# Product tiles of a pair in PE's column halves, with 16 KB stores held back behind loads

## The chip, the cores and the metric

The kernel runs on one core of one Trainium2 chip. Times are device microseconds (us) of that core. "Before" and "after" have four runs each; the experiments ran in three batches, each with its own runs of the kernel before on the same chip. A ratio is the mean time of one kernel's fast runs over the mean of the other's fast runs of the same rounds, so it is not quite the ratio of the medians quoted beside it.

## The reference

Sixteen batches of a product with the second factor transposed, in 32-bit floats:

```python
def setup_inputs():
    batch, m, k, n = 16, 512, 512, 512
    return {"a": randn(batch, m, k), "b": randn(batch, n, k)}   # float32

def reference(a, b):
    return np.matmul(a, b.transpose(0, 2, 1)).astype(np.float32)
```

Each batch reads 2 x 1 MB and writes 1 MB: 33.55 MB in, 16.78 MB out.

## The kernel before

Engines go by the names of the profile: PE is TensorE, which multiplies matrices, ACT is ScalarE, DVE is VectorE, SP is SyncE. SBUF and PSUM are the core's memories; what PE makes goes to PSUM. Batches go in eight pairs, 0 to 7. A load (2 MB, 16 KB per partition) brings one factor of both batches of a pair. DVE casts it to bf16, PE transposes 128 x 128 blocks into PSUM (`tp`), ACT and DVE copy these to SBUF (`ta`, `tb`), PE makes the products in `ps`, ACT copies them to an output ring `ob`, and SP stores them. There are seven load buffers (2 MB) and seven output buffers (1 MB, called halves here: half n is half of pair n // 2). ACT also issues the loads, all but load 1; all stores are issued by SP. The parts that matter:

```python
NL = 7                              # load buffers of 2 MB
NO = 7                              # output buffers of 1 MB
ob = sbuf("ob", [P, NO, J, N], f32)

def landed(n):                      # store n has landed
    return s_st[n % NO], 16 * (n // NO + 1)

def store(n):                       # 1 MB, 8 KB per partition
    nc.sync.wait_ge(s_out, n + 1)
    nc.sync.dma_start(out[n].rearrange("(p j) n -> p j n", j=J), ob[:, n % NO]
                      ).then_inc(landed(n)[0], 16)
...
nc.sync.wait_ge(s_ld[0], 32)        # no store before load 7 has landed
for n in range(batch - 1):
    store(n)
...
for u in range(pairs):              # ACT, in this order
    for ko in range(KO):            # transposes of pair u to ta
        nc.scalar.wait_ge(s_ta, KO * u + ko + 1)
        ...                         # two copies of 512 columns
    for n in (2 * u + NL, 2 * u + NL + 1):
        if n < 2 * pairs:
            load(n, nc.scalar)
    for e in range(2):
        n = 2 * u + e
        if n >= NO:
            nc.scalar.wait_ge(*landed(n - NO))      # output buffer free
        for j in range(J):
            ...                     # ob <- ps, one copy of 512 columns
...
for e in range(2):                  # PE, products of pair u
    for jj in range(0, J, 2):
        ...
        nc.tensor.matmul(ps[:, j, :],                        # 128 rows of batch e
                         ta[:, ko, (e * J + j) * P:(e * J + j + 1) * P],
                         tb[...][:, :, e * HP:(e + 1) * HP], ...)
```

The order on ACT matters below: the copies of pair u+1's transposes stand behind the output copies of pair u, and so behind the wait for an output buffer.

Of the kernel before, what the change touches and what calls it, by code (L numbers as in the profile page):

```python
# [10 lines left out]
def kernel(  # L11
# [6 lines left out]
    nc = tc.nc  # L18
    P = 128
    batch, M, K = a.shape  # L20
    _, N, _ = b.shape
    J = M // P
    KO = K // P
    HP = P // 2
    HK = K // 2
    pairs = batch // 2
    f32 = mybir.dt.float32
    bf16 = mybir.dt.bfloat16
    NL = 7
    NO = 7  # L30



    def sbuf(name, shape, dtype):
        return ctx.enter_context(nc.sbuf_tensor(name, shape, dtype))

    def sem(name):
        return tc.alloc_semaphore(name)

    with tc.tile_critical(no_gpsimd_drain=True):  # L40
        ident = sbuf("ident", [P, P], bf16)
        one = sbuf("one", [P, 1], f32)
        ld = sbuf("ld", [P, NL, 2 * J, K], f32)
        ha, wa, hb, wb = (
            sbuf(name, [P, 2 * J, HK], bf16) for name in ("ha", "wa", "hb", "wb")
        )
        ta = sbuf("ta", [P, KO, 2 * J * P], bf16)
        tb = sbuf("tb", [P, KO, 2 * J * P], bf16)
        ob = sbuf("ob", [P, NO, J, N], f32)
        tp = ctx.enter_context(nc.psum_tensor("tp", [P, 4, 2 * J, P], bf16))  # L50
        ps = ctx.enter_context(nc.psum_tensor("ps", [P, 4, N], f32))

        s_set = sem("s_set")
        s_ld = [sem(f"s_ld{i}") for i in range(NL)]
        s_st = [sem(f"s_st{i}") for i in range(NO)]

        s_go = sem("s_go")
        s_wa = sem("s_wa")
# [6 lines left out]
        s_ea = sem("s_ea")  # L65
        s_eb = sem("s_eb")
        s_mm = sem("s_mm")
        s_pv = sem("s_pv")
        s_out = sem("s_out")
# [5 lines left out]
            out=ident[:], in_=ident[:], compare_op=mybir.AluOpType.not_equal, fill=1.0,  # L75
# [6 lines left out]
        def load(n, engine):  # L82
            u, slot = n // 2, n % NL
            src = (a if n % 2 == 0 else b)[2 * u:2 * u + 2].rearrange(
                "e (p j) k -> (e p) j k", j=2 * J
            )
            engine.dma_start(ld[:, slot], src).then_inc(s_ld[slot], 16)

        def landed(n):
            return s_st[n % NO], 16 * (n // NO + 1)  # L90

        def store(n):
            nc.sync.wait_ge(s_out, n + 1)
            nc.sync.dma_start(
                out[n].rearrange("(p j) n -> p j n", j=J), ob[:, n % NO]
            ).then_inc(landed(n)[0], 16)

        load(0, nc.scalar)
        load(1, nc.sync)
        for n in range(2, NL):  # L100
            load(n, nc.scalar)

        for n in range(2 * pairs):
            nc.gpsimd.wait_ge(s_ld[n % NL], 16 * (n // NL + 1)).then_inc(s_go, 1)  # L104

        nc.sync.wait_ge(s_ld[0], 32)
        for n in range(batch - 1):
            store(n)

        def taker(engine):  # L110
            return lambda s, n: engine.wait_ge(s, n).then_inc(s, -n)  # L111
# [5 lines left out]
        take = taker(nc.vector)  # L117
# [3 lines left out]
        with nc.Fori(0, pairs, engines=[dve]) as u:  # L121
            for x, (h, w, s_c, s_w) in enumerate(
                ((ha, wa, s_ca, s_wa), (hb, wb, s_cb, s_wb))
            ):
                src = ld[:, bass.ds((u * 2 + x) % NL, 1)].rearrange("p o j k -> p (o j) k")
                take(s_go, 1)
                if x == 0:
# [4 lines left out]
                    out=h[:, J:, :], in_=src[:, J:, :HK]  # L132
                ).then_inc(s_c, 1)
                nc.vector.tensor_copy(out=w[:], in_=src[:, :, HK:]).then_inc(s_w, 1)  # L134
            for ko in range(KO):
# [5 lines left out]
                if ko == 1:  # L141
# [3 lines left out]
                    out=tb[:, ko, :],  # L145
                    in_=tp[:, 2 + ko % 2].rearrange("k j p -> k (j p)"),
# [6 lines left out]
        for u in range(pairs):  # L153
            for ko in range(KO):
                nc.scalar.wait_ge(s_ta, KO * u + ko + 1)
                for e in range(2):
                    c = nc.scalar.copy(  # L157
                        out=ta[:, ko, e * J * P:(e + 1) * J * P].rearrange(
                            "k (j p h) -> k j p h", j=J, h=2
                        ),  # L160
                        in_=tp[:, ko % 2, :, e * HP:(e + 1) * HP].rearrange(
                            "k (h j) p -> k j p h", h=2
                        ),
                    )
                c.then_inc(s_ea, 1)


            for n in (2 * u + NL, 2 * u + NL + 1):
                if n < 2 * pairs:
                    load(n, nc.scalar)  # L170
            for e in range(2):
                n = 2 * u + e
                if n >= NO:
                    nc.scalar.wait_ge(*landed(n - NO))
                for j in range(J):
                    nc.scalar.wait_ge(s_mm, J * n + j + 1)
                    c = nc.scalar.copy(  # L177
                        out=ob[:, n % NO, j, :].rearrange("m (p j) -> m p j", j=2 * J),
                        in_=ps[:, j, :].rearrange("m (j p) -> m p j", j=2 * J),
                    )  # L180
                    if e == 0:
                        c.then_inc(s_pv, 1)
                    elif j in (0, J - 1):
                        c.then_inc(s_out, 1)


        pe = nc.tensor.engine
        take = taker(nc.tensor)
        with nc.Fori(0, pairs, engines=[pe]):
            with nc.Fori(0, 2, engines=[pe]):  # L190

                for x, (h, s_c, s_t, s_e) in enumerate(
                    ((ha, s_ca, s_ta, s_ea), (hb, s_cb, s_tb, s_eb))
                ):
                    take(s_c, 1)
                    for g in range(2):
                        take(s_e, 1)
                        for j in range(2 * J):
                            t = nc.tensor.transpose(  # L199
                                tp[:, 2 * x + g, j, :], h[:, j, g * P:(g + 1) * P], ident[:]  # L200
                            )
                            if x == 1 and g == 0 and j == 0:
                                t.then_inc(s_da, 1)
                        t.then_inc(s_t, 1)



            for e in range(2):
                for jj in range(0, J, 2):
                    if e == 1:  # L210
                        take(s_pv, 2)
                    for kk in range(0, KO, 2):
                        for j in (jj, jj + 1):
                            for ko in (kk, kk + 1):
                                if (e, jj, j) == (0, 0, 0) and ko >= 2:
                                    nc.tensor.wait_ge(s_ea, ko - 1)
                                    nc.tensor.wait_ge(s_eb, ko - 1)
                                t = nc.tensor.matmul(  # L218
                                    ps[:, j, :],
                                    ta[:, ko, (e * J + j) * P:(e * J + j + 1) * P],  # L220
                                    tb[:, ko, :].rearrange("k (j p) -> k j p", j=2 * J)[
                                        :, :, e * HP:(e + 1) * HP
                                    ],
                                    start=(ko == 0),
                                    stop=(ko == KO - 1),
                                )
                            if kk == KO - 2:
                                t.then_inc(s_mm, 1)



    with tc.tile_critical(sync_engine=act, no_gpsimd_drain=True):
        for n in range(batch - NO, batch - 1):
            nc.scalar.wait_ge(*landed(n))
    waits = nc.cur_bb.bb.instructions[-1]
    last = nc.sync.dma_start(
        out[batch - 1].rearrange("(p j) n -> p j n", j=J), ob[:, (batch - 1) % NO]
    )
    tc.add_manual_dep(
        last.ins,  # L240
        waits.name,
# [33 lines left out]
```

## Time and profile before

| | before |
|---|---|
| time, median of 4 runs | 124.92 us (124.88 to 124.99) |
| moved | 50.34 MB, mean 409 GB/s over the span |
| PE busy | 73% of the span |
| DMA | nine tenths or more busy in nearly every slice |

Read such a page from the bottom of the hardware up: when the DMA row is full and no engine is, bytes set the time, and an engine matters only if it comes so late that the DMA has nothing to do. These lines of the page are groups of instructions (count | busy us, mean ns of one | idle before, with its cause) and, last, DMA issues (count, KB each, median us from issue to landing):

```profile
L218 PE MATMUL ps<-tb,ta 128*128 128x512 bf16 x256 | 57.8, 379 | 0.5
...
L218 PEld LDWEIGHTS ps<-tb,ta 128*128 128x128 bf16 x256 | 24.1, 98 | 30.6 <-issue 4.0
...
out_dram<-ob SPq DMA_DIRECT2D x16, 1024.0 KB, 25.6
```

From the table of waits of the kernel before (us in total, times, longest):

```profile
ACT ob L177 <- DMA out_dram<-ob: 3.8, 2, 3.1
```

A store takes a median of 25.6 us to land, and yet ACT waits only 3.8 us for one: stores queue deeply, and the ring of seven halves covers it.

### The profile page before, as it was taken

The page shows a single profiled execution, that of the slowest core. Times are in us where ns is not written, and L with a number is a line of the kernel's source. Part 1 is how long each engine was busy: PE and PEld are TensorE (multiplying, and loading weights), DVE is VectorE, ACT ScalarE, POOL GpSimd, SP SyncE. Part 2 cuts the span into 40 slices and gives each one's busy share as a digit, 9 for nine tenths or more (in the row PEclk, how much of TensorE's full clock was granted, in tenths as well). Part 3 has the DMA queues.
Part 4 walks back from the last instruction along what each step waited for, and adds up shares of the span by engine and source line. Part 5 has one row for each costly group of instructions (what it writes and reads, how often), then busy time and mean ns, then how long its engine had stood idle before and what let it go on. Part 6 is the DMA issues. An engine that isn't in the chain of part 4 may idle for free. (4 is left out here: it accounts for less than half of the span.)

```text
span 123.1 us, 2235 instructions
## 1 busy us (share of the span) xinstructions
PE 90.1 (73%) x768; PEld 54.7 (44%) x768; DVE 67.9 (55%) x96; ACT 67.9 (55%) x130; POOL 0.7 (1%) x6
## 2 busy tenths in 40 slices
PE   0000089999999899989998999999699936997000
PEld 0000078447734764575477447644564425542000
DVE  0000598992896589388918983871987039600000
ACT  0400064567945966696589468855865184666000
POOL 2000000000000000000000000000000000000000
PEclk9999999999999999999999999999999999999965
DMA  4999999999999998999999999999999999999991
GB/s 144 394 426 431 447 437 431 426 431 426 426 431 426 426 405 373 453 399 437 407 429 426 463 405 442 437 415 434 423 418 458 399 426 423 431 429 423 426 431 45
DMA packets 4610, 50.34 MB, mean 409 GB/s; under 512 B 513, under 2 KB 513, under 8 KB 513
## 3 DMA queue, kind: packets, MB, share of 16 engines
q10 hardware_dynamic: 2160, 31.46, 60.6%
q1 hardware_dynamic: 2448, 18.88, 36.4%
q14 instruction: 2, 0.01, 0.0%
HBM read 33.55 MB, written 16.78 MB: 409 GB/s over the span
## 5 line engine op out<-in xcount | busy, mean ns | idle before, releaser
L218 PE MATMUL ps<-tb,ta 128*128 128x512 bf16 x256 | 57.8, 379 | 0.5
L177 ACT COPY ob<-ps 128x512 f32<-128x512 f32 x64 | 34.3, 590 | 26.3 <-PE ps L218 22.5
L157 ACT COPY ta<-tp 128x512 bf16<-128x512 bf16 x64 | 33.0, 613 | 15.5 <-PE tp L199 15.0
L218 PEld LDWEIGHTS ps<-tb,ta 128*128 128x128 bf16 x256 | 24.1, 98 | 30.6 <-issue 4.0
L199 PE MATMUL tp<-ident,ha 128*128 128x128 bf16 x256 | 18.5, 224 | 18.8 <-PEq L111 18.3
L199 PEld LDWEIGHTS tp<-ident,ha 128*128 128x128 bf16 x256 | 15.8, 100 | 22.3 <-issue 20.6
L144 DVE COPY tb<-tp 128x1024 bf16<-128x1024 bf16 x32 | 21.2, 685 | 3.6 <-DVEq L111 3.6
L199 PE MATMUL tp<-ident,hb 128*128 128x128 bf16 x256 | 17.5, 223 | 3.8 <-PEq L111 3.5
L199 PEld LDWEIGHTS tp<-ident,hb 128*128 128x128 bf16 x256 | 15.3, 100 | 5.0 <-issue 4.8
L130 DVE CAST ha<-ld 128x1024 bf16 x8 | 5.5, 690 | 14.6 <-POOLq L104 13.8
L139 DVE COPY ha<-wa 128x2048 bf16<-128x2048 bf16 x8 | 5.5, 691 | 12.4 <-DVEq L111 12.4
L130 DVE CAST hb<-ld 128x1024 bf16 x8 | 5.5, 689 | 8.4 <-DVEq L111 8.4
L134 DVE CAST wa<-ld 128x2048 bf16 x8 | 9.8, 1220 | 0.0
L134 DVE CAST wb<-ld 128x2048 bf16 x8 | 9.8, 1220 | 0.0
L131 DVE CAST hb<-ld 128x1024 bf16 x8 | 5.5, 687 | 0.0
L131 DVE CAST ha<-ld 128x1024 bf16 x8 | 5.5, 687 | 0.0
L143 DVE COPY hb<-wb 128x2048 bf16<-128x2048 bf16 x8 | 5.5, 684 | 0.0
L152 ACT ACT_TABLE_LOAD x1 | 1.3, 1283 | 4.1 <-issue 4.1
L74 POOL TENSOR_SCALAR_AFFINE_SELECT ident<-ident 128x128 bf16<-128x128 bf16 x1 | 0.3, 292 | 0.2 <-POOL ident L72 0.2
L72 POOL MEMSET ident<- 128x128 bf16 x1 | 0.2, 204 | 0.5 <-SPq L40 0.5
L152 ACT COPY one<-const-float32-1.0 128x1 f32<-128x1 f32 x1 | 0.2, 191 | 0.0
L259 POOL MEMSET const-bfloat16-1.0<- 128x1 bf16 x1 | 0.1, 102 | 0.0
(3 smaller groups left out, 0.3 us busy)
## 6 DMA issues: line engine op xcount, KB each, us to landing
ld<-in_a_dram ACTq DMA_DIRECT2D x8, 2048.0 KB, 29.3
out_dram<-ob SPq DMA_DIRECT2D x16, 1024.0 KB, 25.6
ld<-in_b_dram ACTq DMA_DIRECT2D x7, 2048.0 KB, 27.1
ld<-in_b_dram SPq DMA_DIRECT2D x1, 2048.0 KB, 12.6
```

What stands on the lines that cost most here:

```text
L74: nc.gpsimd.affine_select(out=ident[:], in_=ident[:], compare_op=mybir.AluOpType.not_equal, fill=1.0, base=0, pattern=[[-1, P]], channel_m ...
L130: nc.vector.tensor_copy(out=h[:, :J, :], in_=src[:, :J, :HK])
L131: nc.vector.tensor_copy(out=h[:, J:, :], in_=src[:, J:, :HK]).then_inc(s_c, 1)
L134: nc.vector.tensor_copy(out=w[:], in_=src[:, :, HK:]).then_inc(s_w, 1)
L139: nc.vector.tensor_copy(out=ha[:], in_=wa[:]).then_inc(s_ca, 1)
L143: nc.vector.tensor_copy(out=hb[:], in_=wb[:]).then_inc(s_cb, 1)
L144: nc.vector.tensor_copy(out=tb[:, ko, :], in_=tp[:, 2 + ko % 2].rearrange("k j p -> k (j p)"),).then_inc(s_eb, 1)
L152: nc.scalar.copy(out=one[:], in_=nc.const_aps.tensor(1.0, (P, 1), f32))
L157: c = nc.scalar.copy(out=ta[:, ko, e * J * P:(e + 1) * J * P].rearrange("k (j p h) -> k j p h", j=J, h=2), in_=tp[:, ko % 2, :, e * HP:(e ...
L177: c = nc.scalar.copy(out=ob[:, n % NO, j, :].rearrange("m (p j) -> m p j", j=2 * J), in_=ps[:, j, :].rearrange("m (j p) -> m p j", j=2 * J),)
L199: t = nc.tensor.transpose(tp[:, 2 * x + g, j, :], h[:, j, g * P:(g + 1) * P], ident[:])
L218: t = nc.tensor.matmul(ps[:, j, :], ta[:, ko, (e * J + j) * P:(e * J + j + 1) * P], tb[:, ko, :].rearrange("k (j p) -> k j p", j=2 * J)[:, ...
```

## The change

The intent is stores of 16 KB per partition instead of 8 KB. For that one partition of `ob` must hold eight consecutive output rows, so both batches of a pair have to be in one product tile: batch 0 in output rows 0 to 63, batch 1 in rows 64 to 127. PE computes them as two products of 64 rows in its two column halves. A pair then leaves as one store of 2 MB, except where the ring of seven halves wraps and at the end. Each of the first four pairs' stores is held until load 2u+8 has landed. Core of the diff, cut:

```diff
+    NS = 5
+    STORES = []
+    for u in range(pairs):
+        if 2 * u % NO == NO - 1 or u == pairs - 1:
+            STORES += [(2 * u,), (2 * u + 1,)]
+        else:
+            STORES += [(2 * u, 2 * u + 1)]
...
-        nc.sync.wait_ge(s_ld[0], 32)
-        for n in range(batch - 1):
-            store(n)
+        for n, halves in enumerate(STORES[:-1]):
+            late = 2 * (halves[0] // 2) + 8
+            if late < 2 * pairs:
+                nc.sync.wait_ge(s_ld[late % NL], 16 * (late // NL + 1))
+            nc.sync.wait_ge(s_out, halves[-1] + 1)
+            store(n).then_inc(landed(n)[0], 16)
...
-                for e in range(2):
-                    c = nc.scalar.copy(out=ta[:, ko, e * J * P:(e + 1) * J * P]..., in_=...)
+                c = nc.scalar.copy(out=ta[:, ko, :], in_=tp[:, ko % 2]...)
...
+                            for e in range(2):
+                                half = slice(e * HP, (e + 1) * HP)
                                 t = nc.tensor.matmul(
-                                    ps[:, j, :],
-                                    ta[:, ko, (e * J + j) * P:(e * J + j + 1) * P],
-                                    tb[:, ko, :]...[:, :, e * HP:(e + 1) * HP],
+                                    ps[half, j % 4, :],
+                                    ta[:, ko, j * P + e * HP:j * P + (e + 1) * HP],
+                                    tb[:, ko, :]...[:, :, half],
```

The resulting stores are (0,1) (2,3) (4,5) (6) (7) (8,9) (10,11) (12,13) (14) (15), by halves.

More of the change, by code (lines that the diff above doesn't have):

```diff
@@ L29 @@
     NL = 7
+    W = 2 * J
     NO = 7
+    NS = 5
[5 more added lines that the diff above has]
+            STORES += [(2 * u, 2 * u + 1)]
+    OF = {h: n for n, halves in enumerate(STORES) for h in halves}
     def sbuf(name, shape, dtype):
@@ L48 @@
         tb = sbuf("tb", [P, KO, 2 * J * P], bf16)
-        ob = sbuf("ob", [P, NO, J, N], f32)
+        ob = sbuf("ob", [P, NO * J, N], f32)
         tp = ctx.enter_context(nc.psum_tensor("tp", [P, 4, 2 * J, P], bf16))
@@ L54 @@
         s_ld = [sem(f"s_ld{i}") for i in range(NL)]
-        s_st = [sem(f"s_st{i}") for i in range(NO)]
+        s_st = [sem(f"s_st{i}") for i in range(NS)]
         s_go = sem("s_go")
@@ L89, in landed @@
         def landed(n):
-            return s_st[n % NO], 16 * (n // NO + 1)
+            return s_st[n % NS], 16 * (n // NS + 1)
         def store(n):
-            nc.sync.wait_ge(s_out, n + 1)
-            nc.sync.dma_start(
-                out[n].rearrange("(p j) n -> p j n", j=J), ob[:, n % NO]
-            ).then_inc(landed(n)[0], 16)
+            halves = STORES[n]
+            u, lo = halves[0] // 2, halves[0] % 2 * J
+            at = halves[0] % NO * J
+            return nc.sync.dma_start(
+                out[2 * u:2 * u + 2].rearrange("e (p w) n -> (e p) w n", w=W)[
+                    :, lo:lo + len(halves) * J, :
+                ],
+                ob[:, at:at + len(halves) * J],
+            )
         load(0, nc.scalar)
@@ L155 @@
                 nc.scalar.wait_ge(s_ta, KO * u + ko + 1)
-                for e in range(2):
-                    c = nc.scalar.copy(
-                        out=ta[:, ko, e * J * P:(e + 1) * J * P].rearrange(
-                            "k (j p h) -> k j p h", j=J, h=2
-                        ),
-                        in_=tp[:, ko % 2, :, e * HP:(e + 1) * HP].rearrange(
-                            "k (h j) p -> k j p h", h=2
-                        ),
-                    )
+                c = nc.scalar.copy(
+                    out=ta[:, ko, :], in_=tp[:, ko % 2].rearrange("k j p -> k (j p)")
+                )
                 c.then_inc(s_ea, 1)
@@ L170 @@
                     load(n, nc.scalar)
-            for e in range(2):
-                n = 2 * u + e
-                if n >= NO:
-                    nc.scalar.wait_ge(*landed(n - NO))
-                for j in range(J):
-                    nc.scalar.wait_ge(s_mm, J * n + j + 1)
-                    c = nc.scalar.copy(
-                        out=ob[:, n % NO, j, :].rearrange("m (p j) -> m p j", j=2 * J),
-                        in_=ps[:, j, :].rearrange("m (j p) -> m p j", j=2 * J),
-                    )
-                    if e == 0:
-                        c.then_inc(s_pv, 1)
-                    elif j in (0, J - 1):
-                        c.then_inc(s_out, 1)
+            for j in range(W):
+                h = 2 * u + j // J
+                if j % J == 0 and h >= NO:
+                    nc.scalar.wait_ge(*landed(OF[h - NO]))
+                nc.scalar.wait_ge(s_mm, W * u + j + 1)
+                c = nc.scalar.copy(
+                    out=ob[:, h % NO * J + j % J, :].rearrange("m (p j) -> m p j", j=W),
+                    in_=ps[:, j % 4, :].rearrange("m (j p) -> m p j", j=W),
+                )
+                if j < J:
+                    c.then_inc(s_pv, 1)
+                elif j in (J, W - 1):
+                    c.then_inc(s_out, 1)
         pe = nc.tensor.engine
@@ L204 @@
                         t.then_inc(s_t, 1)
-            for e in range(2):
-                for jj in range(0, J, 2):
-                    if e == 1:
-                        take(s_pv, 2)
-                    for kk in range(0, KO, 2):
-                        for j in (jj, jj + 1):
-                            for ko in (kk, kk + 1):
-                                if (e, jj, j) == (0, 0, 0) and ko >= 2:
-                                    nc.tensor.wait_ge(s_ea, ko - 1)
-                                    nc.tensor.wait_ge(s_eb, ko - 1)
-                                t = nc.tensor.matmul(
-                                    ps[:, j, :],
-                                    ta[:, ko, (e * J + j) * P:(e * J + j + 1) * P],
-                                    tb[:, ko, :].rearrange("k (j p) -> k j p", j=2 * J)[
-                                        :, :, e * HP:(e + 1) * HP
-                                    ],
+            for jj in range(0, W, 2):
+                if jj >= J:
+                    take(s_pv, 2)
+                for kk in range(0, KO, 2):
+                    for j in (jj, jj + 1):
+                        for ko in (kk, kk + 1):
+                            if j == 0 and ko >= 2:
+                                nc.tensor.wait_ge(s_ea, ko - 1)
+                                nc.tensor.wait_ge(s_eb, ko - 1)
+                            for e in range(2):
+                                half = slice(e * HP, (e + 1) * HP)
+                                t = nc.tensor.matmul(
+                                    ps[half, j % 4, :],
+                                    ta[:, ko, j * P + e * HP:j * P + (e + 1) * HP],
+                                    tb[:, ko, :].rearrange("k (j p) -> k j p", j=W)[:, :, half],
                                     start=(ko == 0),
@@ L226 @@
                                 )
-                            if kk == KO - 2:
-                                t.then_inc(s_mm, 1)
+                        if kk == KO - 2:
+                            t.then_inc(s_mm, 1)
     with tc.tile_critical(sync_engine=act, no_gpsimd_drain=True):
-        for n in range(batch - NO, batch - 1):
+        for n in range(len(STORES) - 1 - NS, len(STORES) - 1):
             nc.scalar.wait_ge(*landed(n))
     waits = nc.cur_bb.bb.instructions[-1]
-    last = nc.sync.dma_start(
-        out[batch - 1].rearrange("(p j) n -> p j n", j=J), ob[:, (batch - 1) % NO]
-    )
+    last = store(len(STORES) - 1)
     tc.add_manual_dep(
```

## The prediction

> **What bounds the kernel now.** I began with the page of the profile: engines, the 40 slices, the queues, the groups.
>
> ```profile
> span 123.1 us, 2235 instructions
> PE 90.1 (73%) x768; PEld 54.7 (44%) x768; DVE 67.9 (55%) x96; ACT 67.9 (55%) x130; POOL 0.7 (1%) x6
> ...
> DMA  4999999999999998999999999999999999999991
> ...
> q10 hardware_dynamic: 2160, 31.46, 60.6%
> q1 hardware_dynamic: 2448, 18.88, 36.4%
> ...
> L177 ACT COPY ob<-ps 128x512 f32<-128x512 f32 x64 | 34.3, 590 | 26.3 <-PE ps L218 22.5
> L157 ACT COPY ta<-tp 128x512 bf16<-128x512 bf16 x64 | 33.0, 613 | 15.5 <-PE tp L199 15.0
> ```
>
> The reader is to see that no compute engine is full (PE leads with 73%), while the DMA row stands at 9 in every slice but the first, one at 8, and the last. The two queues take 60.6 + 36.4 = 97% of the 16 engines' span. The queue q10 carries the loads that ACT issues, q1 the stores and one load. So the kernel is bound by bytes. The chain of waits that ended last covers only some 6% of the span, from 104.9 us on; it tells little here.
>
> The second view is the table of stretches, with the GB/s in its last column.
>
> ```profile
> 24.00:32.00 8.00, 7.61 (x70) 4.73 (x69) 5.48 (x8) 5.95 (x12) 0.00 (x0) 1.00 1.00 428
> ...
> 44.00:52.00 8.00, 7.95 (x51) 3.94 (x49) 5.97 (x8) 4.93 (x11) 0.00 (x0) 1.00 1.00 406
> 52.00:60.00 8.00, 7.55 (x79) 4.94 (x77) 6.66 (x11) 6.15 (x13) 0.00 (x0) 1.00 0.99 421
> ...
> 76.00:84.00 8.00, 7.56 (x65) 4.36 (x62) 5.94 (x9) 5.56 (x11) 0.00 (x0) 1.00 0.98 419
> ...
> 116.00:120.00 4.00, 0.00 (x0) 0.00 (x0) 0.00 (x0) 0.00 (x0) 0.00 (x0) 0.76 1.02 430
> 120.00:121.00 1.00, 0.00 (x0) 0.00 (x0) 0.00 (x0) 0.00 (x0) 0.00 (x0) 0.50 0.30 123
> ```
>
> At 24 to 32 us there are only loads (16 KB packets): 428 GB/s. At 116 to 120 there are only stores (8 KB packets): 430. So packet size alone costs nothing that I can see. With both in flight it is a little lower; my seven stretches of 8 us from 44 to 100 gave 406, 421, 435, 426, 419, 432, 426, mean 424. The transfers end near 120.3 us and 2.8 us of closing work follow.
>
> The third view is the timeline, for the compute's pace and for when loads land.
>
> ```profile
> 33.04 7.29 PE L218 MATMUL ps<-tb,ta 128*128 128x512 bf16 x32
> ...
> 44.51 7.29 PE L218 MATMUL ps<-tb,ta 128*128 128x512 bf16 x32
> ...
> 85.79 0.69 DVE L130 CAST hb<-ld 128x1024 bf16 x1 [3.39 <-DVEq L111]
> ...
> 100.41 0.69 DVE L130 CAST hb<-ld 128x1024 bf16 x1 [4.77 <-DVEq L111]
> ...
> 105.83 7.29 PE L218 MATMUL ps<-tb,ta 128*128 128x512 bf16 x32
> ...
> 113.98 0.33 SPq L236 DMA_DIRECT2D out_dram<-ob  x1
> ```
>
> Fed freely, PE takes 44.51 - 33.04 = 11.47 us a pair: 7.29 of products (228 ns each) and 4.18 of transposes and gaps. A pair's 6.29 MB cost 14.7 us at 427 GB/s, so PE has some 3 us to spare per pair. The two DVE casts that waited show load 13 landing at 85.8 and load 15 at 100.4: 7.31 us a load, 287 GB/s, two thirds of 427. That is what two queues do that alternate packet for packet, 16 KB of load against 8 KB of store.
>
> **What the Trainium skill says.** "DMA: Bandwidth & Descriptors", section "Queues, rings and completion order": each DMA engine goes round its queues by packets. The two-thirds share just worked out agrees. The same page, section "Where 436 GB/s comes from": a ceiling of 435 GB/s. The trace's 426 to 430 are within 2% of it, so no shape of transfer can buy much. "TensorE: Matmul & The Clock Gate", section "Part 3: Packing small matmuls": matmuls in different tiles of the array run at once, with starts some 4 ns apart, three column tiles giving 2.38 times as measured. No matmul of the kernel before is tiled, so this trace can't confirm it. "TensorEngine Tiling (Array Packing)", "Restrictions" and "Key Properties": column tiling disables the fast weight load, and a change of tiling mode drains PE. The trace has no case of either.
>
> **The change part by part.**
>
> *PE.* Each product of 128 output rows becomes two of 64, one per batch, in the two column halves: 64 instead of 32 per pair, each still streaming 512 columns; weight loads double too, with 64 columns each. If halves overlap, a couple takes the 228 ns of one product now; if not, 456. Issue isn't the limit: 16 transposes with their weight loads took 1.05 us, 66 ns each, so a couple needs about 132 ns. Extra: weight changes that aren't hidden (a transpose of 128 columns takes 66 ns and a product of 512 takes 228, so a column costs 162 / 384 = 0.42 ns and the fixed part, weight change included, is 12 ns; doubled, a couple takes 240 ns), and two mode changes a pair, estimated at 0.15 us each. Together d = 32 x 12 ns + 0.3 = 0.7 us a pair at the worse end, about 0.2 if the fixed parts of the halves overlap as well. I choose d = 0.4: 11.9 us a pair.
>
> *How much d PE can take.* Running freely from 33.04 (pair 1), pair 7's products start at 33.04 + 6 x 11.47 = 101.9 us, later by 7d; its last eviction ends 8 + d later (now 105.83 to 113.8). For the DMA not to run dry, the last 1 MB store (2.5 us at 427) must be issued by about 120.3 - 2.5 - 0.8 (issue to first bytes, from the first load's 0.9 to about 1.7) = 117. So 101.9 + 8 + 8d < 117, d < 0.9. My step-by-step reckoning, which includes output buffers, puts the start of the loss near 0.7. Beyond that each microsecond of d costs 8. So 2% slower, 2.5 us, means d of about 1.0 to 1.1: a couple at some 260 ns.
>
> *ACT.* Two copies of 512 columns become one of 1024, 32 fewer instructions. The before pace is about 535 ns back to back, near one column a nanosecond, so one copy of 1024 is about 1.07 us where two took 1.09. No gain worth counting, and ACT is not the bound. Evictions stay 64.
>
> *Stores.* 16 stores of 1 MB become 6 of 2 MB and 4 of 1 MB. Packets on q1: q10's 2160 for 15 loads is 144 each, and 2448 is 17 x 144: one load and 16 stores; now 144 + 10 x 144 = 1584. A packet of 16 KB against one of 16 KB gives the stores half of the engines while both wait, not a third, and the loads 9.8 us each.
>
> *The hold.* Before, the first store waited for load 7 (42.75 us); now pair u's waits for load 2u+8. Reckoned in bytes at 427 GB/s (an estimate): load 8 at about 47 us, then a 2 MB store shares with a load, the following load goes alone, and so on. Stores of pairs 0 to 3 go at about 47, 62, 76, 91; load 15 lands near 98 (before: 100.4); then the remaining stores drain, and pair 7 is done near 113 to 114, as before. At each step the ACT queue holds a load, because loads 9 to 15 are issued one pair's transposes ahead of need, so holding a store empties nothing. Output buffers (7 MB) then bind: the second half of pair 4 waits for pair 1's store until about 73, pair 5's likewise until about 88, so ACT waits on landed stores where now it waits 3.8 us in all. These stall PE in time it has spare.
>
> *Sum.* Bytes are unchanged: 50.34 MB. The mixed phase may go from 424 to 428 if alternation of equal packets, or the spells of loads alone, remove the dip: 56 us x 1% = 0.5 us at most. I take half, 0.25, and set the chance of a late tail against it: 124.9 - 0.25, about **124.7 us**.
>
> **Rivals.** (1) *PE becomes the bound* because column halves don't overlap fully. For it: the fast weight load goes, weight loads double, a couple above 253 ns is enough. Against: the skill's packing numbers and 100 ns or so free in a couple's issue time. A couple at 290 ns makes d about 2 and 133 us; no overlap at all, d = 7.3, makes about 175 us. (2) *The hold makes bubbles*: stores bunch up, output buffers fill, ACT blocks, loads are issued late. For it: ACT will wait more. Against: the byte reckoning shows no moment with both queues empty at d below 0.7. If wrong, 1 to 4 us. (3) *The transfers gain more than I think*: long runs and mostly one direction at a time lift the rate to the 435 of the skill. Then 50.34 MB take 115.7 us instead of some 118.5, and the time is near 122.2. Against it: 16 KB loads alone reach only 428 and 8 KB stores 430.
>
> **Range and chances.** Even rival 3 barely reaches 2% (122.4), so faster gets 0.04. Slower needs a couple above some 260 ns or bubbles over 2.5 us: 0.18. The rest, 0.78, is within 2%. The low end, 123.4, is a mixed phase without the dip and a slightly better rate; the high end, 128.0, is d near 1.2.
>
> **What the profile after will show.** Right: DMA row still at 9, q1 at 1584 packets; 512 products and 1024 PE instructions; the product phase of a free pair within 7.3 to 8 us; loads with a store beside them about 9.8 us apart, alone 4.9; ACT's wait on landed stores above 3.8 us; transfers ending near 120. Wrong: gaps in the DMA row after 80 us (PE or the hold), a product phase above 8.4 us (rival 1), or stretches at 433 GB/s and more while stores and loads mix (rival 3).

## The result, and the profile after

| | before | after |
|---|---|---|
| median | 124.92 us (124.88 to 124.99) | 126.02 us (125.92 to 126.56) |
| ratio of fast runs | | 1.0096, interval 1.0067 to 1.0126 |

So the time is 1% longer: the same within 2%, but clear of noise. The page of the kernel after:

```profile
span 124.8 us, 2712 instructions
...
PE 93.4 (75%) x1024; PEld 65.3 (52%) x1024; DVE 68.0 (54%) x96; ACT 65.6 (53%) x98; POOL 0.7 (1%) x6
...
PEclk9999999999999999999999999999999599999985
DMA  4999999999999999999999999999999999999393
...
q1 hardware_dynamic: 1584, 18.88, 35.7%
...
L234 PE MATMUL ps<-tb,ta 128*64 128x512 bf16 x512 | 58.0, 382 | 0.0
...
L234 PEld LDWEIGHTS ps<-tb,ta 128*64 128x64 bf16 x512 | 32.7, 110 | 22.4 <-issue 3.4
...
out_dram<-ob SPq DMA_DIRECT2D x6, 2048.0 KB, 14.0
```

Twice as many products keep PE busy for the same 58 us, because the two halves of a couple (the two products of 64 rows that make one tile) run at once. In the records of single instructions they start 3 to 4 ns apart in 74 of the 256 couples and 28 to 31 ns apart in the other 182, and couples follow each other every 216 ns, as single products of 128 rows did before. The DMA row has something new: a 3 in the third slice from the end. The stretches of half a microsecond there (last columns: DMA share, GB/s):

```profile
114.50:115.00 0.50, 0.50 (x8) 0.35 (x6) 0.00 (x0) 0.50 (x2) 0.00 (x0) 1.00 0.99 426
...
115.50:116.00 0.50, 0.50 (x8) 0.30 (x5) 0.00 (x0) 0.06 (x1) 0.00 (x0) 1.00 0.17 66
...
117.00:117.50 0.50, 0.50 (x9) 0.29 (x5) 0.00 (x0) 0.34 (x1) 0.00 (x0) 1.00 0.09 33
```

From about 115.2 to 117.7 us the DMA has next to nothing to move, while PE (first number after the width) is busy with the last pair. So the outputs of pair 7 come too late. The timeline shows where that begins (start, duration, instruction; in brackets idle before it and who ended it):

```profile
45.40 7.22 PE L234 MATMUL ps<-tb,ta 128*64 128x512 bf16 x64
...
57.00 7.22 PE L234 MATMUL ps<-tb,ta 128*64 128x512 bf16 x64
...
63.54 2.05 ACT L191 COPY ob<-ps 128x512 f32<-128x512 f32 x4 [2.08 <-DMA out_dram<-ob]
...
77.92 2.05 ACT L191 COPY ob<-ps 128x512 f32<-128x512 f32 x4 [4.46 <-DMA out_dram<-ob]
...
81.03 0.61 PE L213 MATMUL tp<-ident,ha 128*128 128x128 bf16 x8 [2.91 <-PEq L132]
...
82.39 1.06 PE L213 MATMUL tp<-ident,hb 128*128 128x128 bf16 x16
...
83.38 7.23 PE L234 MATMUL ps<-tb,ta 128*64 128x512 bf16 x64
...
92.58 2.05 ACT L191 COPY ob<-ps 128x512 f32<-128x512 f32 x4 [4.75 <-DMA out_dram<-ob]
...
97.41 1.91 PE L213 MATMUL tp<-ident,hb 128*128 128x128 bf16 x16
...
99.25 7.48 PE L234 MATMUL ps<-tb,ta 128*64 128x512 bf16 x64
...
111.11 7.22 PE L234 MATMUL ps<-tb,ta 128*64 128x512 bf16 x64
```

Left alone, a pair takes 57.00 - 45.40 = 11.60 us (before: 11.47). But three times ACT stands still until a store has landed: 2.08, 4.46 and 4.75 us, before the second halves of pairs 3, 4 and 5. ACT works in order, so the copies of the next pair's transposes wait behind that, and PE waits for those (2.91 us before 81.03). Products of pair 5 begin 14.4 us after those of pair 4 (69.00), pair 6's 15.9 us after that. Pair 7's start at 111.11 us, where before they started at 105.83. The last store is issued at 119.2 instead of 113.98.

Not all of this is waiting. The row PEclk has a 5 in the slice near 98 us: by the trace's clock records PE was granted half its clock from 96.65 to 100.06 us, just when pair 6's transposes came. Those marked 97.41 took 1.91 us where the same ones of pair 5 took 1.06. From the first transposes after the wait to the first product pair 6 took 3.56 us (95.69 to 99.25) where pair 5 took 2.35 (81.03 to 83.38), and its products 7.48 where others took 7.22. So some 1.5 of the 5.3 us by which pair 7 is late are the clock's in this run; whether the wait brought the half clock on isn't shown.

The waits table says the same (ACT's line answers to the one of before):

```profile
ACT ob L191 <- DMA out_dram<-ob: 11.3, 3, 4.8
```

The packet records say why the stores land late. For the stores that held ACT up:

| store of pair | issued | first packet | last packet ends | landed |
|---|---|---|---|---|
| 0 | 47.40 | 51.37 | 62.47 | 63.51 |
| 1 | 64.14 | 67.65 | 77.22 | 77.89 |
| 2 | 78.77 | 82.34 | 91.83 | 92.56 |

The load beside each takes 9.9 to 10.3 us (alone 5.4 to 5.5), so the stores do get half of the engines, as predicted. But with loads queued, 3.5 to 4.0 us pass from issue to the first packet, and 0.7 to 1.0 us from the last packet to the landing. At the end, with no load queued, the first of these was 0.84 and 1.06 us.

Last, the time from first to last packet, by what the 16 engines did in the mean. The typical packet took 611 ns for 16 KB and 309 ns for 8 KB; "slow" is what packets took beyond that, and "idle" includes engines that finish before the last one:

| profiled run | typical | slow | idle | sum |
|---|---|---|---|---|
| before (124.88 us) | 117.76 | 1.27 | 0.65 | 119.68 |
| after (126.56 us) | 117.42 | 1.97 | 1.99 | 121.38 |

Of the 1.70 us more, 1.34 are idle and 0.70 slow packets (0.6 of it in load packets that began within 5 us of the first store's issue); the longer runs give back 0.34. This profiled run was the slowest of its four, 0.5 us above their median, so the terms are of that one run, and the half clock above has its part in the idle.

### The profile page after: what moved, and what is told of

Read it like the earlier page. It is cut to its first block, busy times and chain, and to the rows that moved or that the text cites. A ratio compares the mean times of both kernels' runs of the same rounds, so it can differ in the third digit from the quotient of the medians.

```text
span 124.8 us, 2712 instructions
## 1 busy us (share of the span) xinstructions
PE 93.4 (75%) x1024; PEld 65.3 (52%) x1024; DVE 68.0 (54%) x96; ACT 65.6 (53%) x98; POOL 0.7 (1%) x6
## 3 DMA queue, kind: packets, MB, share of 16 engines
q1 hardware_dynamic: 1584, 18.88, 35.7%
## 5 line engine op out<-in xcount | busy, mean ns | idle before, releaser
L234 PE MATMUL ps<-tb,ta 128*64 128x512 bf16 x512 | 58.0, 382 | 0.0
L234 PEld LDWEIGHTS ps<-tb,ta 128*64 128x64 bf16 x512 | 32.7, 110 | 22.4 <-issue 3.4
L177 ACT COPY ta<-tp 128x1024 bf16<-128x1024 bf16 x32 | 30.8, 1029 | 14.4 <-PE tp L213 14.4
L213 PE MATMUL tp<-ident,ha 128*128 128x128 bf16 x256 | 19.5, 233 | 23.9 <-PEq L132 23.9
L213 PEld LDWEIGHTS tp<-ident,ha 128*128 128x128 bf16 x256 | 16.3, 104 | 28.3 <-issue 28.2
L213 PE MATMUL tp<-ident,hb 128*128 128x128 bf16 x256 | 18.9, 233 | 1.0 <-PEq L132 0.5
L213 PEld LDWEIGHTS tp<-ident,hb 128*128 128x128 bf16 x256 | 16.8, 105 | 1.8 <-issue 1.8
```

What stands on the lines that cost most here:

```text
L177: c = nc.scalar.copy(out=ta[:, ko, :], in_=tp[:, ko % 2].rearrange("k j p -> k (j p)"))
L213: t = nc.tensor.transpose(tp[:, 2 * x + g, j, :], h[:, j, g * P:(g + 1) * P], ident[:])
L234: t = nc.tensor.matmul(ps[half, j % 4, :], ta[:, ko, j * P + e * HP:j * P + (e + 1) * HP], tb[:, ko, :].rearrange("k (j p) -> k j p", j=W) ...
```

## The experiments

The theory: held stores land so late that ACT waits for output buffers and pair 7 comes late. The rivals: column halves slow PE; 2 MB stores cost, whatever the hold. All results in one table; "before" is the median in the same batch.

| run | us, median | before | ratio (95% interval) |
|---|---|---|---|
| hold undone | 134.97 | 125.02 | 1.0757 (1.0711 to 1.0803) |
| hold for load 2u+7 | 125.88 | 125.02 | 1.0063 (1.0041 to 1.0085) |
| hold for 2u+9 | 129.90 | 125.02 | 1.0401 (1.0367 to 1.0436) |
| column halves, 1 MB stores | 125.57 | 125.02 | 1.0039 (1.0016 to 1.0062) |
| before, with the hold | 125.28 | 125.20 | 1.0006 (0.9977 to 1.0036) |
| before, longer PE program | 125.02 | 125.20 | 0.9992 (0.9969 to 1.0015) |
| 2u+7 for four pairs | 125.80 | 125.20 | 1.0040 (1.0015 to 1.0066) |
| the same, first store split | 125.44 | 125.20 | 1.0019 (0.9995 to 1.0044) |
| before, store addresses of after | 125.15 | 125.09 | 1.0006 (0.9983 to 1.0030) |
| column halves, store addresses of before | 125.45 | 125.09 | 1.0026 (1.0003 to 1.0050) |
| column halves, 1 MB stores, again | 125.47 | 125.09 | 1.0031 (1.0006 to 1.0055) |

### The hold undone

```diff
-            late = 2 * (halves[0] // 2) + 8
-            if late < 2 * pairs:
-                nc.sync.wait_ge(s_ld[late % NL], 16 * (late // NL + 1))
+            if n == 0:
+                nc.sync.wait_ge(s_ld[0], 32)
```

> The change with its hold undone: only the first store waits for a load (load 7), as before the change. Rival 'the hold itself is the loss': 124.6 to 125.0 us, and ACT's waits on landed stores fall under 4 us. My theory: the hold is there because a 16 KB packet gives the stores half of the DMA engines instead of a third; without it every load from load 8 on takes about 10 us instead of 7.4, load 15 lands near 111 us instead of 98, pair 7 ends some 8 us later, and the time is 128 to 134 us, with a gap in the DMA row before the end. Rival 'column halves slow PE': unchanged, 126.0.

Measured 134.97 us, a little past my range and far from both rivals. No wait of ACT on stores is left in its table of waits, yet the stretches show a long DMA gap while PE makes the last pair:

```profile
116.00:120.00 4.00, 4.00 (x40) 3.89 (x38) 2.76 (x5) 1.78 (x2) 0.00 (x0) 0.50 0.03 12
120.00:124.00 4.00, 4.00 (x41) 2.23 (x41) 1.30 (x2) 1.53 (x4) 0.00 (x0) 0.99 0.00 0
```

Load 15 landed at 113.49 us (before: 100.07), since loads with a 2 MB store beside them took about 10.3 us instead of 7.4; pair 7's products started at 120.43. The column before the last two shows that PE had half its clock there: from the cast of load 15 to the first product 6.6 us passed where it was 5.4 before, some 1.2 us more, about as much as I was out by. So 16 KB stores need a hold: their packets take half of the engines, and the loads, which the last pair waits for, pay.

### One load earlier, and one later

```diff
-            late = 2 * (halves[0] // 2) + 8
+            late = 2 * (halves[0] // 2) + 7          # and + 9 in the other run
```

> The change with each pair's store held for load 2u+7 instead of 2u+8, so about 5 us earlier. My theory: the loss is that held stores land 4 to 5 us later than I reckoned (some 4 us from issue to the first packet while loads are queued), so that the second halves of pairs 3 to 5 wait for output buffers 2.1, 4.5 and 4.8 us, ACT stands in the way of the next transposes, and pair 7 is 5 us late. One load earlier takes these waits away: ACT's wait on landed stores falls from 11.3 us to under 4, pair 7's products start at 104 to 107 us instead of 111, no gap in the DMA row at the end, 124.3 to 124.9 us. Rival 'column halves slow PE' and rival '2 MB stores are to blame whatever the hold': 125.7 to 126.2, unchanged.

> The dose the other way: held for load 2u+9. My theory: each store some 5 us later than in the change, so three second halves (pairs 3, 4, 5) wait some 5 us longer in sum on the path and pair 7 comes 4 to 6 us later: 129.5 to 132 us with a DMA gap of 6 to 8 us near the end. Rival 'the hold does not matter, PE or store size does': 126.0.

Later (2u+9) it was 129.90 us, as the theory said. ACT's timeline shows the first wait grown from 2.08 to 6.62 us and the other two somewhat shorter, the sum now 13.7 us:

```profile
67.49 2.05 ACT L191 COPY ob<-ps 128x512 f32<-128x512 f32 x4 [6.62 <-DMA out_dram<-ob]
82.28 2.05 ACT L191 COPY ob<-ps 128x512 f32<-128x512 f32 x4 [4.06 <-DMA out_dram<-ob]
96.70 2.05 ACT L191 COPY ob<-ps 128x512 f32<-128x512 f32 x4 [3.01 <-DMA out_dram<-ob]
```

Pair 7's products began at 113.77 us, 2.7 us later than in the change, where I had written 4 to 6. Two stretches of half clock (69.97 to 73.39 and 87.04 to 90.45 us) lay on transposes of pair 4 and on pair 5's transposes and products, so here too a part of the lateness is the clock's. The gap in the DMA was smaller than I had written, some 2.5 us near 118 to 120.4, in a profiled run of 128.65 us, the fastest of its four.

Earlier (2u+7) the waits shrank to 4.5 us and pair 7 came at 107.06, about as expected, but the time, 125.88 us, lay in the rivals' range. By the time alone my expectation failed. Its table of waits and timeline, and then the stretches, which show a new gap:

```profile
ACT ob L191 <- DMA out_dram<-ob: 4.5, 2, 3.6
...
107.06 7.22 PE L234 MATMUL ps<-tb,ta 128*64 128x512 bf16 x64
...
101.00:101.50 0.50, 0.50 (x8) 0.35 (x6) 0.00 (x0) 0.00 (x0) 0.00 (x0) 1.00 0.21 82
101.50:102.00 0.50, 0.50 (x8) 0.09 (x4) 0.46 (x1) 0.41 (x1) 0.00 (x0) 1.00 0.16 66
```

With 2u+7, pair 4 is held as well, for load 15. That is the last load: while its store waits for it, nothing else is in the queues once it lands, and the store's first packet came 0.84 us after its issue at 101.21.

### The earlier hold for four pairs, and a smaller first store

```diff
-            if late < 2 * pairs:
+            if halves[0] < J * 2:                    # pairs 0 to 3 only
...
-        if 2 * u % NO == NO - 1 or u == pairs - 1:
+        if 2 * u % NO == NO - 1 or u in (0, pairs - 1):   # second run only
```

> The change held for load 2u+7, but pairs 0 to 3 alone: with load 2u+7 for pair 4 as well, that pair's store waited for load 15, the last, and the DMA engines stood idle for about 0.9 us near 101 us. My theory: that gap goes and the rest stays (the longer fetch, slower load packets when the first 2 MB store starts): 125.0 to 125.5 us, 0.4 to 0.8 under the 125.88 with pair 4 held. Rival 'column halves or 2 MB stores cost 0.9 us whatever the hold': 125.9.

> As the one before, with pair 0's store in two of 1 MB. In the traces load packets next to the first store are slow, 0.85 to 1.0 us a DMA engine in sum where the first store is 2 MB and 0.4 us where it is 1 MB. If the size of the first store makes that, this saves about 0.4 us: 124.6 to 125.1. If it is chance or belongs to something else, it is as the one before.

The gap near 101 us is gone (426 to 451 GB/s in each microsecond from 99 to 103), and ACT's wait on stores is 3.2 us, less than before the change. The median, 125.80 us, is 0.3 above my range and 0.1 under the rival's number, with a batch in which before itself read 125.20. The ratio fell from 1.0063 to 1.0040, with intervals that overlap, so the gap's worth is not shown by the times. What the times do show is that against the change as made (1.0096, lowest end 1.0067) this hold is better (highest end 1.0066, though measured in different batches), and that what is left equals the column halves alone (1.0039, next section).

Splitting the first store gave 1.0019. Slow packets fell from 1.82 to 1.56 us in the mean; the times of the two runs, 125.30 to 125.97 and 125.24 to 125.79, overlap. It points the way expected and settles nothing.

### The column halves alone

The change with all stores of 1 MB and only the first held for load 7.

```diff
-        if 2 * u % NO == NO - 1 or u == pairs - 1:
-            STORES += [(2 * u,), (2 * u + 1,)]
-        else:
-            STORES += [(2 * u, 2 * u + 1)]
+        STORES += [(2 * u,), (2 * u + 1,)]           # NS = 7
...
+            if n == 0:                               # in place of the hold
+                nc.sync.wait_ge(s_ld[0], 32)
```

> The column halves and the one-piece ACT copies of the change, but 16 stores of 1 MB in 8 KB runs, only the first held (load 7), as before. My theory: PE's pair takes 11.60 us instead of 11.47, which PE has to spare, so 124.7 to 125.2 us, the same as before the change; no gap in the DMA row. Rival 'column halves slow PE and cost the microsecond': 125.8 to 126.3.

> The column halves with 1 MB stores once more, on the same chip as the two above, to compare them with: 0.3 to 0.5 % over before if the first result holds.

125.57 us, ratio 1.0039, and 1.0031 when repeated: between my range and the rival's, and a real 0.3 to 0.4%. PE's pace is not what sets it, as the last pair's products show:

```profile
106.76 7.22 PE L230 MATMUL ps<-tb,ta 128*64 128x512 bf16 x64
```

They start 0.9 us later than before (105.83): half of that came with load 15 (cast at 100.88 instead of 100.41), half with a stretch of half clock from 102.24 to 105.65 us. But the last store, issued at 114.84, still waited 3.16 us for its first packet behind earlier ones, so the queue never ran dry. I looked instead at how far the DMA engines end out of step. By the completion events of the last store, its slowest engine came 2.08 us after the median engine, and 1.66 us in the repeat; before, 1.35 us. But in "before, with the hold", which has no column halves and costs nothing that shows (1.0006), it came 1.67 us after, so this lag is not shown to be the cost.

### What in the column halves costs it

Traces with column halves have a 16 KB instruction fetch at 53 to 55 us that takes one DMA engine 0.93 us (1.08 in one); the trace of before has only one of 8 KB, 0.51 us. So I suspected program length, and gave the kernel before a longer PE program for the same work:

```diff
-            with nc.Fori(0, 2, engines=[pe]):
+            for _ in range(2):                       # transposes written out
```

> The kernel before with PE's inner loop over the transposes written out, so that the same work is done by a PE program 64 instructions longer, as long as that of the column halves. Theory: the column halves cost their 0.4 % (125.57 against 125.02) by program length: all traces with them have one 16 KB instruction fetch near 53 us that holds one DMA engine for 0.93 us, which the trace of before lacks, and that engine finishes last, some 0.7 us further behind the others. Then this run has that fetch too and takes 125.3 to 125.7 us. Rival 'the column halves cost it by PE's 0.13 us a pair or by the way of the stores' 8 KB runs': no such fetch here, 124.8 to 125.1 us.

The 16 KB fetch appeared (at 29.4 us, 1.07 us long), and the time did not move: 0.9992, slowest engine 1.38 us behind at the end. The suspicion in that form has fallen: such a fetch is not enough. Next came the store addresses, since 1 MB stores in the new layout write 8 KB runs at a 16 KB stride. Two kernels with wrong results cross them over:

```diff
 # before, with the addresses of after
-                out[n].rearrange("(p j) n -> p j n", j=J), ob[:, n % NO]
+                out[n // 2 * 2:n // 2 * 2 + 2].rearrange("e (p w) n -> (e p) w n", w=2 * J)[
+                    :, n % 2 * J:(n % 2 + 1) * J, :], ob[:, n % NO]
 # column halves, with the addresses of before
-                out[2 * u:2 * u + 2].rearrange("e (p w) n -> (e p) w n", w=W)[...],
+                out[halves[0]].rearrange("(p j) n -> p j n", j=J),
```

> Wrong result on purpose. The kernel before, with its 16 stores of 1 MB written to the addresses of the column-halves form: 8 KB runs at a stride of 16 KB over two batches. The run with column halves and 1 MB stores took 0.4 % more than before, and in its trace the two slowest DMA engines finish 1.4 and 2.1 us after the median engine (before: 0.8 and 1.35). Theory 'the address pattern of the stores throws the DMA engines out of step': 125.4 to 125.8 us here, with a lag near 2 us. Theory 'it belongs to the PE side, or to the longer programs and their fetches': the same as before, within 0.2 %.

> Wrong result on purpose, the mirror of the one above: column halves, but 1 MB stores to contiguous 8 KB runs as before. Address pattern to blame: the same as before, within 0.2 %. PE side or programs to blame: 0.3 to 0.6 % over before, lag of the slowest engine near 2 us.

The addresses do nothing that shows: 1.0006 with them on the kernel before (slowest engine 1.49 us behind), 1.0026 without them on the column halves (1.88 us). A half clock near the end isn't enough either: the first of these had one from 102.50 to 105.91 us, where the column runs had theirs. So the 0.3% goes with the compute side of the column form, to which ACT's one-piece copies belong. Neither PE's pace, nor the addresses, nor a longer PE program alone carries it; by what path it comes stays open.

### The hold alone

The kernel before, 1 MB stores, with nothing of the change but the hold:

```diff
-        nc.sync.wait_ge(s_ld[0], 32)
         for n in range(batch - 1):
+            late = 2 * (n // 2) + 8
+            if late < 2 * pairs:
+                nc.sync.wait_ge(s_ld[late % NL], 16 * (late // NL + 1))
             store(n)
```

> The kernel before, with nothing of the change but its hold: the stores of pair u, still 1 MB each, wait for load 2u+8. By my reckoning the 8 KB packets still share one to two with the loads, the halves land one after the other, one second half (pair 5) waits some 2 to 3 us for a buffer and pair 7 is 1 to 2 us late, which the queued stores cover: 124.9 to 125.5 us. Rival 'a hold for load 2u+8 costs the microsecond with any kind of store': 126.0 or more, with a gap in the DMA row.

125.28 us, ratio 1.0006. ACT's wait on stores doubled to 7.8 us and the queues still covered it. So the hold for load 2u+8 costs nothing that shows by itself; it cost time together with column halves and stores of 2 MB. I read this as the 1 MB stores freeing a pair's first half earlier, while a 2 MB store frees both at its end; no run has this hold with column halves and 1 MB stores, so that reading is not shown.

## Why the prediction was right or wrong

The measured 126.02 us lies in the range of 123.4 to 128.0 and in the class "within 2%". The small gain of 0.25 us I had put in the middle was a loss of 1.1. So the number held by the width of the range and not by the sum: one step of the sum failed, and its cost was small enough to stay inside.

- **Bound.** Right. Bytes still set the time, and the packet records leave little: 117.4 of the 121.4 us from first to last packet are plain transfer. But the gain I had put on the mixed phase didn't come: its seven stretches from 44 to 100 us gave 420 GB/s in the mean, against 424 before and the 428 hoped for, with 377 from 44 to 52 us, where the load packets were slow.
- **PE.** Right, and better than chosen. d, the extra time of a pair on PE, was 11.60 - 11.47 = 0.13 us against my 0.4. (My 228 ns a product, and the fixed part of 12 ns drawn from it, came of a mean that holds the last product's tail; products start every 216 ns.) The starts some 4 ns apart of "TensorE: Matmul & The Clock Gate", "Part 3: Packing small matmuls", are there in 74 couples of 256, and the others start 28 to 31 ns apart; either way the couple costs what one product did, a full factor of two. Of the two statements taken from the tiling page, the lost fast weight load fits weight loads of 64 columns that took 110 ns in the mean where 128 columns took 98, which doesn't prove it; and draining at the changes of mode can't have cost more than the 0.13 us a pair, unless something else became faster.
- **Stores get half.** Right: loads with a store beside them took 9.9 to 10.3 us against the 9.8 predicted (the next load started 9.3 to 9.7 us after, and 4.9 after a load alone), q1 has the 1584 packets counted. Arbitration by packets, as "DMA: Bandwidth & Descriptors", "Queues, rings and completion order" has it, fits 8 KB and 16 KB stores alike.
- **The hold: this step failed.** I wrote that pair 7 is "done near 113 to 114, as before" and that "the byte reckoning shows no moment with both queues empty at d below 0.7". The order of events was right, down to the second halves of pairs 4 and 5 that wait for a landing (pair 3's, which waited 2.08 us, I had not seen). The mis-sized term is the time at which a held store lands. The waits ended at 77.9 and 92.6 us, not 73 and 88. For 2.1 and 2.8 us of that the stores were issued late, because loads 10 and 12, which release them, landed at 64.13 and 78.75 us and not near 62 and 76. For the rest a store took 13.8 us from issue to landing (16.1 the first), not the 11 and 12 between my own dates: 3.5 to 4.0 us passed to the first packet, where my estimate for the end of the kernel had 0.8, read off the first load in an empty system, and 0.7 to 1.0 us from the last packet to the landing. So pair 7's last store went out at 119.2 us and the DMA stood nearly idle for about 2.5 us, in this run with some help of the half clock. That is rival 2 of the prediction; its cost, 0.7 us between this hold (1.0096) and the one for 2u+7 on four pairs (1.0040), is a little under its 1 to 4. The three holds (2u+7, 2u+8, 2u+9: ratios 1.0063, 1.0096, 1.0401) show that the moment of release is a lever; the landing time was not varied alone.
- **Packet size.** I wrote that it "costs nothing that I can see". It costs 2 x 309 - 611 = 7 ns for two packets of 8 KB against one of 16 KB, 0.34 us in all: real, and too small to be seen in GB/s by stretch.
- **Not foreseen.** The column form costs 0.3 to 0.4% even with the old stores. I had nothing for it in the sum; its path is open.

So of the 1.0%, roughly a third goes with the column halves (0.26 to 0.39 points in three runs) and the rest with held 2 MB stores that land too late. No version here beats the kernel before.

## What to carry to other kernels

When a transfer is held back on purpose, count its time to landing as the queues will be then: waiting behind what is already queued, sharing, and completing, not as one transfer in an empty system. Ask next who needs the buffer it frees, and what stands behind that engine in program order: here three waits of ACT, 11.3 us in sum, made the last pair some 4 us late, beside what the clock did. In this kernel, bound by bytes, longer runs gained 7 ns for each 16 KB, so first work out whether such a gain can pay for what the new layout needs.

## What the Trainium skill lacked or had wrong

- "DMA: Bandwidth & Descriptors", "Latency and other measured facts", gives about 600 ns to the first byte for transfers issued as these are. With loads queued on the other queue, 3.4 to 4.4 us passed from a store's issue to its first packet where no store was ahead of it; with no load queued, 0.83 to 1.06 us. The page has no first-byte figure for a busy system.
- The same page gives the arbitration by packets but not what follows for a kernel: 8 KB store packets against 16 KB loads got a third of the bytes, 16 KB ones half, and undoing the hold cost 7.6%.
- "TensorEngine Tiling (Array Packing)" has no measurement of two column halves in a long run of products. Here 64-row couples of 512 columns came every 216 ns, as single 128-row products did.
- No page has a figure for how far DMA engines drift out of step: at the last store the slowest engine came 1.35 to 1.67 us after the median engine in the four kernels without column halves, 1.66 to 2.18 us in the five with them whose queues stayed full, and 0.08 to 0.77 us in the four whose queues had run dry, the change itself among them (0.65).
